# A fused gMLP / RWKV-7 layer on one core: the first superblock's modulation sums and the spatial weights change places with their neighbours

## The chip, the cores and the metric

The kernel runs on one core of one Trainium2 chip. The metric is device microseconds (us) of one execution. A core has TensorE (PE; its weight loads are shown as PEld), VectorE (DVE), ScalarE (ACT), GpSimd (POOL), and SyncE (SP), whose queue issues every DMA of this kernel.

## The reference, cut to what matters

x is 4096 x 1024. A conditioning vector c gives shift, scale and gate; h = x(1+scale)+shift is projected by one matrix w_in; columns 0 to 1535 feed head group A (u, v, gate), the rest head group B.

```python
shift, scale, gate = split(silu(c) @ w_ada + b_ada)
h = x * (1 + scale) + shift
p = h @ w_in
# group A: 8 groups of 64, chunks of 128
u = gelu(p[:, :512]);  v = layer_norm(gelu(p[:, 512:1024]));  g = silu(p[:, 1024:1536])
w_m = where(causal, w_spatial, 0)
v = einsum('gts,bcsgd->bctgd', w_m, v) + b_spatial
out_a = u * v * g
# group B: token shift, decay from tanh(wd) @ w_up, rate from ad @ a_up, RWKV-7 scan, group norm, silu gate
y = layer_norm(ALPHA * x + gate * (concat(out_a, out_b) @ w_out))
```

## The kernel before, in words

The sequence is cut into 16 superblocks of T = 256 tokens. Every float32 operand of a dense product is held as two rounded parts, hi and lo: `split` casts the source to hi on ACT and subtracts hi from the source on POOL or DVE. A dense block is 8 steps of k; one step is a matmul of 512 columns (L370, weight hi against x hi and lo) and one of 256 (L371, weight lo against x hi).

**Stage one** (0 to about 866 us, lines 456 to 664) runs head group A and the gate and decay columns of group B for all superblocks, with their weights resident. Superblock 0 also loads those weights. Its opening works on the input in halves of k: `first_half(a)` issues the loads of four 1 MB pieces of w_ada (`wa`), two x tiles and one 1 MB piece of w_in (`ust`); `second_half(a)` splits `ust` into the u weights, forms the sums silu(c) @ w_ada with `ada_sum` (16 small matmuls of L329 per 512 columns, a copy by DVE at L491, 8 matmuls of L493 that turn the row into columns of `pmod`), builds scale and shift in `mod`, and modulates and splits the x tiles. `group_a(0)` allocates one PSUM tile for each of the four u blocks, runs k = 0 to 3 of all four (`dense`), then calls `second_half(1)`, then runs k = 4 to 7.

The generator `weights` is advanced one step beside each step of `group_a(0)`: it loads the gate weights (`w_g`, four blocks), then the v weights (two 1 MB pieces `vst`, split into `wv`), then the `w_gb` blocks and `w_wd`, and last the spatial weights: a load of `wm` (512 KB), a mask on POOL (`affine_select`, L545), eight broadcast loads of b_spatial into `cb` (L549, called `bsp` in the rows) and 16 matmuls into `pR` (L553), which make the constant part of the spatial bias. After the u blocks, `group_a` runs the four gate blocks, two v products `psv` (L598 to L600), the `w_gb` blocks, `w_wd`, and the spatial product `pM` (L638).

In stage one the framework's scheduler chooses each engine's order from the order of the program and its own model of readiness; each engine then runs its queue strictly in order. All DMAs wait in SP's queue in order too.

**Stage two** (to about 2180 us) runs head group B twice over the 16 superblocks, two head pairs at a time (`ph` 0 and 1). The order of PE, DVE, ACT and POOL is written out at build time by a list planner, `Weave`: streams yield operations, each has a modelled cost, and the one that can start first is emitted next. A load's modelled due time is set by `W.load`. `dense` (line 861) calls `setup(ph)` at the first superblock of each `ph`: it loads w_up and a_up into two tiles taken from the two-buffer ring `pv` that the token shift also uses, casts them (`wua`) and subtracts. **The output projection** follows to the end.

Of the kernel before, what the change touches and what calls it, by code (L numbers as in the profile page):

```python
# [11 lines left out]
F32 = mybir.dt.float32  # L12
F32R = mybir.dt.float32r
AF = mybir.ActivationFunctionType
ALU = mybir.AluOpType
# [4 lines left out]
P = 128  # L20
# [189 lines left out]
def hybrid_layer(ctx: ExitStack, tc: tile.TileContext, x, xT, w_ada, b_gate, w_in, cols,  # L210
                 consts, wspT, b_sp, w_up, a_up, w_out, ln_g, ln_b, out):
    nc = tc.nc
    v, s, g, pe = nc.vector, nc.scalar, nc.gpsimd, nc.tensor
# [84 lines left out]
    def slices(hls):  # L298
        return [hl[:, :, k] for hl in hls for k in range(2)]
# [165 lines left out]
    with ExitStack() as actx:  # L465
# [20 lines left out]
        def ada_sum(q, parts):  # L486
            pq = ps_m.tile([P, 512], F32, tag="m", name="pq")
            for k in range(KD):
                group_row(pq, sg1, k, parts[k // 4][:, k % 4])
            rows = apool.tile([P, 512], F32, tag="wst", name="rows", bufs=3)  # L490
            v.tensor_copy(rows, pq)  # L491
            for mm in range(4):
                pe.matmul(pm[:, q * 4 + mm:q * 4 + mm + 1], rows[:, mm * P:(mm + 1) * P], row32,  # L493
                          start=True, stop=True)
# [8 lines left out]
            ld(st, w_in[a * 512:(a + 1) * 512, 0:512].rearrange("(k p) c -> p k c", p=P))  # L503
            half[a] = wa, xs, st

        def second_half(a):
            wa, xs, st = half[a]
            for b in range(4):
                split(wu[b][:, 0, 4 * a:4 * a + 4], wu[b][:, 1, 4 * a:4 * a + 4], st[:, :, b * P:(b + 1) * P], v)
            for n, q in enumerate((2 + a, a)):  # L510
                ada_sum(q, wa[n])
            sc, sh = slice(8 + 4 * a, 12 + 4 * a), slice(4 * a, 4 * a + 4)
            v.scalar_tensor_tensor(mod[:, sc], pm[:, sc], 1.0, V[:, V_BA + sc.start:V_BA + sc.stop], op0=ALU.add,
                                   op1=ALU.add)
            v.tensor_tensor(mod[:, sh], pm[:, sh], V[:, V_BA + sh.start:V_BA + sh.stop], op=ALU.add)
            return [modulate(2 * a + n, x_, (v, g)[n]) for n, x_ in enumerate(xs)]
# [7 lines left out]
        def weights():  # L524
            for b in range(4):
                wgt.append(load_w(2 * DA + b * P, f"w_g{b}", None if b < 3 else w2, (g, v)[b % 2], (None, apool)[b % 2]))
                yield
            vst = []
            for r in range(2):
                t_ = w2.tile([P, 4, DA], F32, tag="w", name=f"vst{r}")  # L530
                ld(t_, w_in[r * 512:(r + 1) * 512, DA:2 * DA].rearrange("(k p) c -> p k c", p=P))
                vst.append(t_)
            for k in range(KD):
                split(wv[:, 0, k], wv[:, 1, k], vst[k // 4][:, k % 4], (g, v)[k % 2])
            yield
            for b in range(4):
                wgb.append(load_w(NA + 1536 + b * P, f"w_gb{b}", w2, (g, v)[b % 2], (None, apool)[b % 2]))
                yield
            wwd.append(load_w(NA + 2048, "w_wd", w2))
            yield  # L540
            ones = apool.tile([P, 64], F32, name="ones", bufs=1)
            g.memset(ones, 1.0)
            ld(wm, wspT)

            g.affine_select(wm, wm, pattern=[[0, 8], [1, P]], compare_op=ALU.is_ge, fill=0.0, base=0,  # L545
                            channel_multiplier=-1)
            for b in range(4):
                for gi in range(2):
                    ld(cb[64 * gi:64 * gi + 64, b], b_sp[2 * b + gi:2 * b + gi + 1].partition_broadcast(64))  # L549
            pR = ps_m.tile([P, 4, P], F32, tag="m", name="pR")  # L550
            for b in range(4):
                for gi in range(2):
                    pe.matmul(pR[64 * gi:64 * gi + 64, b], ones, wm[:, 2 * b + gi], start=True, stop=True)  # L553
            for b in range(4):
                v.scalar_tensor_tensor(cb[:, b], pR[:, b], col(V_LB, b), cb[:, b], op0=ALU.mult, op1=ALU.add)
            yield

        def group_a(i):
# [7 lines left out]
            if i:  # L566
                h = load_all(i)
                yield
                for b in range(4):
                    gelu_u(gemm(h, wu[b]))  # L570
                    yield
            else:
                pus = [(ps_d if b < 2 else ps_s).tile([P, 2, T], F32, tag="ddss"[b], name="psd") for b in range(4)]
                for b in range(4):
                    dense(pus[b], slices(hl0), wu[b], 0, 4)
                hl0.extend(second_half(1))
                h = slices(hl0)
                yield
                for b in range(4):
                    dense(pus[b], h, wu[b], 4, KD)  # L580
                    gelu_u(pus[b])
                    yield
                keep_parts(0, hl0)
# [199 lines left out]
    with ExitStack() as bctx:  # L783
# [21 lines left out]
        def rsqrt_b(dst, src, bias_):  # L805
            yield ac.activation(dst, src, AF.Ln, bias=bias_)
            yield ac.activation(dst, dst, AF.Exp, scale=-0.5)

        def setup(ph):

            wua = W.tile(tp, [P, 4, 256], F32R, "wua", 1)
            yield gp.memset(wua[:, 2:4].bitcast(F32), 0.0)
            for q, src in enumerate((w_up, a_up)):
                r_ = slice(64 * q, 64 * q + 64)
                up = W.tile(tp, [P, 257], F32, "pv", 2, "up")[:, 0:256]
                for r in range(2):
                    W.load(up[64 * r:64 * r + 64], src[:, ph * 256:(ph + 1) * 256])
                yield ac.copy(wua[:, q], up)
                yield gp.tensor_tensor(wua[r_, 2 + q], up[r_], wua[r_, q].bitcast(F32), op=ALU.subtract)
            R[ph] = wua  # L820
# [40 lines left out]
        def dense(hs):  # L861
            u, p = divmod(hs, 2)
            ph, i = divmod(u, NSB)
            if p == 0:
                if ph not in R:
                    yield from setup(ph)
                units[u] = {}
                wd = W.tile(tp, [P, 2, T], F32R, "wd", 1)
                W.load(wd.bitcast(F32), wds[i])
                for _ in state["h"][1]:  # L870
                    pass
                state["cur"] = state["h"][0]
                state["side"] = iter(())
                if u == NSB - 1:
                    state["side"] = load_b1()
                elif u == NU - 1:
                    state["side"] = load_out()
            wua, h, n = R[ph], state["cur"], 2 * ph + p
            blocks = [("k", 4 + n), ("r", n), ("v", 8 + n)]

            for group in ([blocks[:1], blocks[1:]] if p else [[z_] for z_ in blocks]):
                pss = [W.tile(ps_d, [P, T], F32, "d", 3, "psd") for _ in group]
                fresh = len(group) > 1 and u + 1 < NU
                if fresh:
                    state["h"] = reload_parts((u + 1) % NSB)
                for k in range(KD):
                    hi, lo = h[k]
                    for (nm, blk), ps in zip(group, pss):
                        w = R[ph, nm, p]
                        yield [mm.matmul(ps, w[:, 0, k], hi, start=(k == 0), stop=False),  # L890
                               mm.matmul(ps, w[:, 0, k], lo, start=False, stop=False),
                               mm.matmul(ps, w[:, 1, k], hi, start=False, stop=(k == KD - 1))]
                    if k % 2 and fresh:
                        next(state["h"][1], None)
                for (nm, blk), ps in zip(group, pss):
                    t_ = W.tile(tp, [P, T], F32, nm, 2, nm + "t")
                    units[u][nm, p] = t_
                    W.spawn(shift_b(hs, nm, ps, blk, t_, n), 1.5)
                    next(state["side"], None)
                if nm == "k" and p == 0:  # L900
                    pw = []
                    for q in range(2):
                        pw.append(W.tile(ps_d, [P, 2, T], F32, "d", 3, "pw"))
                        yield [mm.matmul(pw[q][:, j], wua[:, q + 2 * z_, j * P:(j + 1) * P], wd[:, q],
                                         start=(z_ == 0), stop=(z_ == 1)) for j in range(2) for z_ in range(2)]
                    units[u]["sa"] = sas[u % 2]
                    W.spawn(rates(u, sas[u % 2], pw), 1.5)
                elif late and W.ready[late[0][1].tensor.name][0] <= W.clock["pe"]:
                    yield from put_late(ps_d, "d", 3)
            if p == 1:  # L910
                for _ in state["side"]:
                    pass
# [356 lines left out]
```

## Time and profile before

| | us |
|---|---|
| three runs | 2526.94, 2514.21, 2527.01; median 2526.94 |
| the profiled execution | 2518.34, span 2516.3 |
| busy: PE / DVE / ACT / POOL | 2382.3 / 1587.8 / 1266.3 / 761.0 |
| mean granted TensorE clock | 0.983 of full |

PE is busy for 95% of the span, so the time that can be won without removing matmuls is PE's idle time and the time that it runs at the lower of its two clocks. The timeline shows one instruction or a merged run of the same kind per line: start, duration, engine, line, operation, operands, count, and in brackets how long the engine was idle before it and what ended the wait.

### The profile page before, as it was taken

How to read it: one execution, taken by the hardware profiler on the slowest of the kernel's cores; microseconds unless marked ns; L12 is line 12 of the kernel's file. 1: busy time of each engine (PE TensorE's matmuls, PEld its weight loads, DVE VectorE, ACT ScalarE, POOL GpSimd, SP SyncE). 2: the span in 40 equal slices, each digit the busy share in tenths (PEclk: the TensorE clock that was granted, in tenths of full speed). 3: DMA queues.
4: the chain of work that ended last, by engine and by line, in shares of the span. 5: the costliest groups of instructions: out<-in, count | busy, mean ns of one | idle time of the engine just before them, and what ended most of it. 6: DMA issues, size and time to landing. Idle time of an engine off the chain costs nothing.

```text
span 2516.3 us, 57908 instructions
## 1 busy us (share of the span) xinstructions
PE 2382.3 (95%) x22676; PEld 2081.1 (83%) x22676; DVE 1587.8 (63%) x4205; ACT 1266.3 (50%) x2946; POOL 761.0 (30%) x1417
## 2 busy tenths in 40 slices
PE   7999999999999899999999989999999988899998
PEld 4778888888888798888888888888888887688887
DVE  4444545554344268778788777777877777555555
ACT  3444544454445565666666656566665555211111
POOL 2322433232222333332323333333333233222221
PEclk9999999999999999999999999999999899999999
DMA  8533455443223523222222342222212124344442
GB/s 299 172 122 122 149 178 180 159 147 113 72 72 105 168 77 90 75 71 85 60 86 71 123 137 64 86 69 77 90 56 85 56 77 161 110 147 143 150 148 95
DMA packets 182074, 286.14 MB, mean 114 GB/s; under 512 B 14500, under 2 KB 123172, under 8 KB 180008
## 3 DMA queue, kind: packets, MB, share of 16 engines
q1 hardware_dynamic: 181800, 282.44, 34.6%
q8 instruction: 178, 2.92, 0.5%
q14 instruction: 96, 0.79, 0.1%
HBM read 188.00 MB, written 94.38 MB: 112 GB/s over the span
## 4 chain that ended last, share of the span: by engine, by line
PE 60%; DVE 17%; ACT 7%; issue 4%; DMA 3%; POOL 2%; SPq 1%; DVEq 0%; POOLq 0%; ACTq 0%
PE pso L1221 13%; PE psd L166 12%; PE psd L370 9%; PE psd L371 5%; PE pU L166 3%; PE pC L166 3%; PE pA L166 2%; DVE big L166 2%; PE psv L598 2%; PE psv L600 2%; PE psv L599 2%; DVE X L166 2%; DVE tmp L166 2%; DVE S L166 1%; PE pY L166 1%
## 5 line engine op out<-in xcount | busy, mean ns | idle before, releaser
L1221 PE MATMUL pso<-wo,hx 128*128 128x512 f32 x1440 | 330.5, 391 | 1.8 <-POOL hx L1221 1.3
L1221 PEld LDWEIGHTS pso<-wo,hx 128*128 128x128 f32 x1440 | 270.3, 188 | 60.5 <-POOL hx L1221 1.7
L166 PE MATMUL psd<-hx,w_v 128*128 128x256 f32 x1512 | 251.0, 293 | 11.7 <-DVE kt L166 5.5
L166 PE MATMUL psd<-hx,w_r 128*128 128x256 f32 x1512 | 251.1, 292 | 2.7 <-issue 1.4
L166 PE MATMUL psd<-hx,w_k 128*128 128x256 f32 x1512 | 237.5, 298 | 4.9 <-DVE rt L166 4.9
L166 PEld LDWEIGHTS psd<-hx,w_v 128*128 128x128 f32 x1512 | 204.6, 192 | 17.7 <-DVE kt L166 7.1
L381 DVE TENSOR_TENSOR sum<-psd,sum 128x256 f32<-128x256 f32 x208 | 87.4, 421 | 195.1 <-ACT sum L380 195.0
L166 PEld LDWEIGHTS psd<-hx,w_r 128*128 128x128 f32 x1512 | 205.2, 191 | 6.2 <-DVE kt L166 2.1
L166 PEld LDWEIGHTS psd<-hx,w_k 128*128 128x128 f32 x1512 | 202.0, 197 | 7.3 <-DVE rt L166 6.0
L370 PE MATMUL psd<-hx,w_u 128*128 128x512 f32 x512 | 187.7, 409 | 6.2 <-ACT w_u L258 5.8
L370 PE MATMUL psd<-hx,w_gb 128*128 128x512 f32 x512 | 183.4, 400 | 0.5 <-DVE sum L381 0.5
L370 PE MATMUL psd<-hx,w_g 128*128 128x512 f32 x512 | 182.1, 399 | 0.5 <-DVE sum L381 0.5
L1221 POOL TENSOR_TENSOR hx<-hst,hx 128x512 fp32r<-128x512 f32 x58 | 81.8, 1412 | 221.5 <-ACT hx L1221 219.7
L371 PE MATMUL psd<-hx,w_u 128*128 128x256 f32 x512 | 145.8, 285 | 1.2 <-DVE w_u L259 1.2
L371 PE MATMUL psd<-hx,w_gb 128*128 128x256 f32 x512 | 144.9, 283 | 0.0
L371 PE MATMUL psd<-hx,w_g 128*128 128x256 f32 x512 | 143.8, 281 | 0.0
L166 ACT ACTIVATE pv<-psd,V 128x256 f32<-128x256 f32 x192 | 89.6, 474 | 98.1 <-PE psd L166 95.8
L166 POOL COPY halo<-pv 128x1 f32<-128x1 f32 x192 | 39.2, 205 | 315.0 <-ACT pv L166 308.0
L1221 DVE SCALAR_TENSOR_TENSOR z<-z,pso 128x512 f32<-128x512 f32 x60 | 41.2, 687 | 146.6 <-PE pso L1221 146.5
L380 ACT COPY sum<-psd 128x256 f32<-128x256 f32 x208 | 75.7, 365 | 107.4 <-PE psd L371 107.1
L370 PEld LDWEIGHTS psd<-hx,w_u 128*128 128x128 f32 x512 | 98.2, 192 | 34.0 <-ACT w_u L258 6.0
L259 POOL TENSOR_TENSOR hx<-hst,hx 128x512 fp32r<-128x512 f32 x62 | 79.7, 1294 | 128.9 <-ACT hx L258 128.9
(222 smaller groups left out, 5906.0 us busy)
## 6 DMA issues: line engine op xcount, KB each, us to landing
hx<-xhl SPq DMA_DIRECT2D x126, 512.0 KB, 4.1
xhl<-hx SPq DMA_DIRECT2D x64, 512.0 KB, 2.9
hst<-in_xT_dram SPq DMA_DIRECT2D x64, 256.0 KB, 3.5
hst<-oT SPq DMA_DIRECT2D x64, 256.0 KB, 2.9
z<-in_x_dram SPq DMA_DIRECT2D x32, 512.0 KB, 3.5
out_dram<-z SPq DMA_DIRECT2D x32, 512.0 KB, 2.6
wst<-in_w_in_dram SPq DMA_DIRECT2D x42, 256.0 KB, 3.6
wa<-in_w_ada_dram SPq DMA_DIRECT2D x8, 1024.0 KB, 12.0
```

The lines of the kernel that those rows point to most:

```text
L166: fn(*a, **k)
L259: eng.tensor_tensor(lo, src, hi.bitcast(F32), op=ALU.subtract)
L370: pe.matmul(ps, w[:, 0, k], both, start=(k == 0), stop=(k == KD - 1), skip_group_check=True)
L371: pe.matmul(ps[:, 0], w[:, 1, k], both[:, 0], start=False, stop=(k == KD - 1), skip_group_check=True)
L380: s.copy(t_, ps[:, 1])
L381: v.tensor_tensor(t_, ps[:, 0], t_, op=ALU.add)
L598: pe.matmul(ps, hi[:, js], wv[:, 0, k], start=(k == 0), stop=False)
L599: pe.matmul(ps, hi[:, js], wv[:, 1, k], start=False, stop=False)
L600: pe.matmul(ps, lo[:, js], wv[:, 0, k], start=False, stop=(k == KD - 1))
L1221: fn(*a, **k)
```

## The change

Three edits. (1) `second_half` takes a callable `beside` that it calls after the two `ada_sum`s and before `mod` is built; `group_a(0)` runs k = 0 to 3 of u blocks 0 and 1 before `second_half(1)` and hands it k = 0 to 3 of blocks 2 and 3. (2) In `weights`, the load of `wm`, its mask, and the eight loads of `cb` move from the last step to the step of the v weights, ahead of the two `vst` loads; the `pR` matmuls stay where they were. (3) `setup` no longer loads w_up and a_up: a new `fetch_low(ph)` loads them into one tile of their own, called at unit 0 for `ph` 0 and at unit 15, one unit before it is needed, for `ph` 1.

```diff
-        def second_half(a):
+        def second_half(a, beside=lambda: None):
...
             for n, q in enumerate((2 + a, a)):
                 ada_sum(q, wa[n])
+            beside()
             sc, sh = slice(8 + 4 * a, 12 + 4 * a), slice(4 * a, 4 * a + 4)
...
+            ones = apool.tile([P, 64], F32, name="ones", bufs=1)
+            g.memset(ones, 1.0)
+            ld(wm, wspT)
+
+            g.affine_select(wm, wm, pattern=[[0, 8], [1, P]], compare_op=ALU.is_ge, fill=0.0, base=0,
+                            channel_multiplier=-1)
+            for b in range(4):
+                for gi in range(2):
+                    ld(cb[64 * gi:64 * gi + 64, b], b_sp[2 * b + gi:2 * b + gi + 1].partition_broadcast(64))
             vst = []
...
             wwd.append(load_w(NA + 2048, "w_wd", w2))
             yield
-            ones = apool.tile([P, 64], F32, name="ones", bufs=1)
-            g.memset(ones, 1.0)
-            ld(wm, wspT)
...
             pR = ps_m.tile([P, 4, P], F32, tag="m", name="pR")
...
-                for b in range(4):
-                    dense(pus[b], slices(hl0), wu[b], 0, 4)
-                hl0.extend(second_half(1))
+
+                part = slices(hl0)
+                for b in range(2):
+                    dense(pus[b], part, wu[b], 0, 4)
+
+                def beside():
+                    for b in range(2, 4):
+                        dense(pus[b], part, wu[b], 0, 4)
+
+                hl0.extend(second_half(1, beside))
...
+        def fetch_low(ph):
+            up = W.tile(tp, [P, 2, 256], F32, "up", 1)
+            for q, src in enumerate((w_up, a_up)):
+                for r in range(2):
+                    W.load(up[64 * r:64 * r + 64, q], src[:, ph * 256:(ph + 1) * 256])
+            R["up", ph] = up
+
         def setup(ph):
...
-                up = W.tile(tp, [P, 257], F32, "pv", 2, "up")[:, 0:256]
-                for r in range(2):
-                    W.load(up[64 * r:64 * r + 64], src[:, ph * 256:(ph + 1) * 256])
+                up = R["up", ph][:, q]
...
             if p == 0:
+
+                if u in (0, NSB - 1):
+                    fetch_low((u + 1) // NSB)
                 if ph not in R:
```

## Rows read from the trace of the kernel before

**Rows 1.** Windows: length, busy us (instructions) by engine, clock, DMA share, GB/s.
```profile
100.00:200.00 100.00, 99.19 (x540) 77.93 (x539) 43.38 (x139) 39.87 (x77) 18.79 (x33) 1.00 0.36 119
...
1460.00:1475.00 15.00, 10.56 (x134) 9.18 (x132) 7.36 (x23) 8.05 (x24) 7.09 (x16) 0.77 0.63 198
...
1700.00:1800.00 100.00, 97.29 (x1427) 89.44 (x1414) 80.21 (x228) 68.61 (x174) 36.12 (x83) 1.00 0.25 76
1800.00:1900.00 100.00, 91.57 (x1284) 84.05 (x1282) 78.82 (x228) 60.29 (x154) 31.93 (x74) 0.97 0.26 79
```

**Rows 2.** Timeline of PE in the opening, 12 to 43 us.
```profile
29.99 0.46 PE L370 MATMUL psd<-hx,w_u 128*128 128x512 f32 x1
...
32.92 2.78 PE L329 MATMUL pq<-wa,sg 128*32 128x512 f32 x24
...
38.59 1.05 PE L493 MATMUL pmod<-K,rows 128*128 128x1 f32 x8 [0.88 <-DVE rows L491]
42.55 0.79 PE L370 MATMUL psd<-hx,w_u 128*128 128x512 f32 x1 [2.91 <-ACT w_u L258]
```

**Rows 3.** Timeline of ACT just before that.
```profile
41.88 2.18 ACT L258 CAST w_u<-ust 128x512 fp32r<-128x512 f32 x4
```

**Rows 4.** Timeline of SP, 0 to 130 us (time and total length of a run of issues).
```profile
46.25 2.62 SPq L269 DMA_DIRECT2D wst<-in_w_in_dram  x2
48.92 1.05 SPq L531 DMA_DIRECT2D vst<-in_w_in_dram  x2
...
71.16 0.50 SPq L543 DMA_DIRECT2D wm<-in_wspT_dram  x1
71.71 6.40 SPq L549 DMA_DIRECT2D bsp<-in_b_sp_dram  x8
```

**Rows 5.** DMA issues, 0 to 130 us: count, size of each, us from issue to landing.
```profile
vst<-in_w_in_dram SPq DMA_DIRECT2D x2, 1024.0 KB, 8.6
wm<-in_wspT_dram SPq DMA_DIRECT2D x1, 512.0 KB, 6.5
```

**Rows 6.** Timelines of POOL, ACT and DVE, 55 to 79 us, in order of time.
```profile
55.31 2.99 POOL L259 TENSOR_TENSOR wv<-vst,wv 128x512 fp32r<-128x512 f32 x2 [2.19 <-ACT wv L258]
...
58.43 2.17 ACT L258 CAST wv<-vst 128x512 fp32r<-128x512 f32 x4
...
59.58 3.38 DVE L259 TENSOR_TENSOR wv<-vst,wv 128x512 fp32r<-128x512 f32 x2 [0.73 <-ACT wv L258]
62.89 0.74 DVE L381 TENSOR_TENSOR sum<-psd,sum 128x256 f32<-128x256 f32 x2
...
78.08 1.09 POOL L545 TENSOR_SCALAR_AFFINE_SELECT wm<-wm 128x1024 f32<-128x1024 f32 x1
```

**Rows 7.** Timeline of PE, 63 to 99 us.
```profile
63.35 0.49 PE L598 MATMUL psv<-wv,hx 128*128 128x512 f32 x1 [0.99 <-DVE sum L381]
...
74.66 0.40 PE L370 MATMUL psd<-hx,w_gb 128*128 128x512 f32 x1
79.23 1.97 PE L553 MATMUL pR<-wm,ones 128*64 128x128 f32 x16 [4.18 <-POOL wm L545]
...
84.72 0.40 PE L370 MATMUL psd<-hx,w_gb 128*128 128x512 f32 x1
...
93.91 0.39 PE L370 MATMUL psd<-hx,w_wd 128*128 128x512 f32 x1
...
96.83 1.97 PE L638 MATMUL pM<-wm,vg 128*64 128x128 f32 x32
```

**Rows 8.** Timelines of ACT, SP and PE around the two calls of `setup`.
```profile
874.00 0.40 ACT L166 CAST wua<-up 128x256 fp32r<-128x256 f32 x1 [7.87 <-DMA up<-in_w_up_dram]
...
1464.38 1.11 SPq L84 DMA_DIRECT2D up<-in_w_up_dram  x2
...
1468.80 0.40 ACT L166 CAST wua<-up 128x256 fp32r<-128x256 f32 x1 [3.11 <-DMA up<-in_w_up_dram]
...
1471.06 1.22 PE L166 MATMUL pU<-rhs,yt 128*128 128x128 f32 x4 [3.07 <-ACT rhs L166]
```

More of the change, by code (lines that the diff above doesn't have):

```diff
@@ L540, in weights @@
             yield
-            ones = apool.tile([P, 64], F32, name="ones", bufs=1)
-            g.memset(ones, 1.0)
-            ld(wm, wspT)
-            g.affine_select(wm, wm, pattern=[[0, 8], [1, P]], compare_op=ALU.is_ge, fill=0.0, base=0,
-                            channel_multiplier=-1)
-            for b in range(4):
-                for gi in range(2):
-                    ld(cb[64 * gi:64 * gi + 64, b], b_sp[2 * b + gi:2 * b + gi + 1].partition_broadcast(64))
             pR = ps_m.tile([P, 4, P], F32, tag="m", name="pR")
@@ L573, in group_a @@
                 pus = [(ps_d if b < 2 else ps_s).tile([P, 2, T], F32, tag="ddss"[b], name="psd") for b in range(4)]
-                for b in range(4):
-                    dense(pus[b], slices(hl0), wu[b], 0, 4)
-                hl0.extend(second_half(1))
+                part = slices(hl0)
[5 more added lines that the diff above has]
+                hl0.extend(second_half(1, beside))
                 h = slices(hl0)
@@ L812, in setup @@
             yield gp.memset(wua[:, 2:4].bitcast(F32), 0.0)
-            for q, src in enumerate((w_up, a_up)):
+            for q in range(2):
                 r_ = slice(64 * q, 64 * q + 64)
-                up = W.tile(tp, [P, 257], F32, "pv", 2, "up")[:, 0:256]
-                for r in range(2):
-                    W.load(up[64 * r:64 * r + 64], src[:, ph * 256:(ph + 1) * 256])
+                up = R["up", ph][:, q]
                 yield ac.copy(wua[:, q], up)
```

## The prediction

> **What bounds the kernel now.** I read the windows first, to see where PE is not the limit, then PE's timeline for its idle brackets, then the queues that release those waits. From 100 to 200 us PE is busy 99.2 of 100 us [rows 1], and the later windows of stage one look the same, so stage one is bound by PE: a microsecond won in the first 100 us is not swallowed before stage two. The reader should look for three places where PE stands still. At 42.55 PE waits 2.91 us for the cast of the u weights, the end of the modulation chain [rows 2]. At 79.23 it waits 4.18 us for the mask of the spatial weights [rows 7]. At 1471.06, in the start of the second half of stage two, it waits 3.07 us behind ACT, which itself stood 3.11 us for the load of w_up [rows 8]. The change has one edit for each.
>
> **Edit 1, the modulation sums.** Blocks 2 and 3 of the first half-products run from 29.99 to 32.92, 2.93 us [rows 2]. The sums start at 32.92 and their last matmul ends at 38.59 + 1.05 = 39.64; the modulation, the casts (that of the u weights at 41.88 [rows 3]) and so the wait of 2.91 us follow. If PE does the sums right after block 1, the chain starts 2.93 us earlier and the two blocks fill its gaps; PE restarts at 42.55 - 2.93 = 39.62. The blocks then cover the idle time almost wholly (2.91 + 0.88 of idle against 2.93 of work), so PE should not fall to the lower clock either. What that clock costs I take from the other restart: after the 4.18 us of waiting, PE runs at half speed from the end of pR at 81.2 to 84.72 [rows 7], 3.5 us, which costs half of it, 1.75 us. Here part of it hides under the wait for the splits of the u weights, so I take 1.1 (bounds 0 and 1.75). Edit 1 brings 2.93 + 1.1 = 4.0 us at the end of the u blocks. No engine gets more work, and the transfers that the sums need were issued long before; that they have landed at 29.99 no row shows, only that they had by 32.92, where PE does not wait. If they had not, the gain is 0 (rival C).
>
> **Edit 2, the spatial weights.** What it removes: PE's wait of 4.18 us; pR at half speed (16 matmuls in 1.97 us, where pM does 32 of the same shape in 1.97 us [rows 7], so 0.98 too much); and the slow restart of 1.75. Together 6.9 us. The mask itself takes 1.09 us on POOL [rows 6]; in its new place it stands before the splits of the v weights, where POOL sat idle for 2.19 us, so it is free there, and uncovered it costs 1.09. The wm load takes 6.5 us to land [rows 5] and has some 20 us until pR. After it nothing on PE is late: the next block after psv has its weights split by then (L370 at 74.66 had begun before the wait [rows 7]).
>
> What it adds: nine issues on SP ahead of the two `vst` loads. One wm issue takes 0.50 us and the eight broadcasts 6.40 us [rows 4]; that last figure holds waits. The bounds are nine times 0.50 = 4.5, and 0.50 + 6.40 = 6.9. Behind them in SP's queue stand vst, the stores of the split x and all w_gb loads. The two `wst` loads before vst end at 48.87 [rows 4]; they wait for splits that move 2.93 us earlier with edit 1, so vst is issued between 46.0 + 4.5 = 50.5 and 52.9, against 48.92: 1.6 to 4.0 us later, although the rest of the stage is earlier. The second vst piece is cast at 58.43 and the last of its splits ends at 59.58 + 3.38 = 62.96 [rows 6]; this becomes 64.6 to 67.0. PE would be ready for psv at 63.35 - 0.99 - 4.0 = 58.4. So edit 2 takes back part of edit 1. The two psv products run from 63.35 to 74.66, 11.3 us for 48 matmuls, 0.236 each; psv 0 needs 5.65 and ends at 69.0 now. If it follows the splits as they come, only its last step of three matmuls, 0.7, is left after the last split: it ends at 65.3 to 67.7, a gain of 1.3 to 3.7. I take the middle, 2.5, for edit 1 and the late vst together.
>
> The Trainium skill (DMA: Bandwidth & Descriptors, section "Issuing engines are not separate DMA queues") says that the sequencer's time to start a DMA is usually small beside the DMA. By that rule the nine issues would cost little, edit 1's 4.0 us would survive whole, and the sum would be 1.5 higher. The rows do not agree for these eight: 6.40 us of issuing for 32 KB each.
>
> **Edit 3, w_up and a_up.** At the second `setup` the load is issued at 1464.38 and ACT waits until 1468.80; the cast stands ahead of the scan's copies on ACT, so PE waits 3.07 us [rows 8]. Loaded one unit earlier, this wait goes. The window 1460 to 1475 has a clock of 0.77 [rows 1]: 0.23 x 15 / 0.5 = 6.9 us at half speed, of which about 4.5 were idle, so at most 1.2 more comes back. I take 3.1, bounds 1.5 (half is lost to the next wait) and 4.3. The four loads are the same, only earlier. At the first `setup` ACT waits 7.87 us until 874.00 for the same loads [rows 8], but there nothing is issued earlier, since `fetch_low(0)` is called just ahead of `setup(0)`: I count 0. The `pv` ring is freed of two tiles. But the planner sees other due times from its first step on, so the order of all four engines in stage two can come out differently; no row prices that. The nearest are two neighbouring windows of the same work, in which PE is busy 97.3 and 91.6 us of 100 [rows 1]: 5.7 us between a good and a bad stretch of the same plan. I take 0, with 5 either way.
>
> **Sum.** 2.5 + 6.9 + 3.1 = 12.5 us. The profiled execution took 2518.34, so 2505.8 on that scale. It lies 8.6 below the median of the three runs and 4.1 above the lowest; the mean of all four executions is 2521.6, and 2521.6 - 12.5 = 2509. I predict 2510. A difference under 0.5%, 12.6 us, is about what a measurement of this kernel cannot tell from no change; the forecast sits right at that border.
>
> **Rivals.**
> A, the queue on DVE does not follow. Now the sums of gate blocks 1 and 2 (62.89) stand behind DVE's splits of the v weights, and psv 0 waits for the PSUM tile that they free [rows 6, 7]. If this order stays and vst comes 1.6 to 4.0 us later, psv 0 starts at 65.0 to 67.4 instead of 63.35, after some 7 us of idle, with a slow restart of 1.75: a loss of 3.4 to 5.8, middle 4.6. Total -4.6 + 6.9 + 3.1 = 5.4 gained: 2512.9 on the profile's scale. For it: it is the order of now. Against it: the framework chose that order with vst early, and chooses again. The same loss comes if the vst data queue behind wm's 512 KB on the DMA engines. The Trainium skill (DMA: Bandwidth & Descriptors, section "Queues, rings and completion order") says that descriptors on one engine are consumed in ring order, which would put them there; no row shows the two in flight together.
> B, everything is kept. wm and the broadcasts go out in a gap where SP waits anyway, vst is not late, and edit 1 keeps 4.0 and the 0.99 us at 63.35; edit 3 brings 4.3. 4.0 + 1.0 + 6.9 + 4.3 = 16.2: 2502.1. Against it: the framework would have had such gaps for wm before, and did not use them (wm at 71.16 [rows 4]).
> C, edit 1 does not do what it says: the framework's model finds the w_ada pieces not ready after block 1 and lets blocks 2 and 3 go first, as now. Then vst is 4.5 to 6.9 late, psv 0 ends at 68.2 to 70.6 against 69.0, a loss of 0.4 in the middle; -0.4 + 6.9 + 3.1 = 9.6: 2508.7.
> D, slower: the planner's new order is worse. It decides once it loses more than 12.5, a little over twice the 5.7 us between the two windows; three such stretches would cost 17 and end 4.6 above now: 2522.9. For it: the first due times change at the first unit, and 32 units follow. Against it: only two calls of `setup` are changed, and the streams and their costs stay.
>
> **How the numbers follow.** Forecast 0.48, A 0.20, B 0.12, C 0.10, D 0.10. The forecast's own range is 1.3 + 5.15 + 1.5 = 8.0 (edit 2 without the 1.75 of the clock) to 3.7 + 6.9 + 4.3 = 14.9 gained, so 2503.4 to 2510.4 on the profile's scale. The runs lie 4.1 below to 8.7 above that scale: 2499 to 2519; A ends at 2521.6 with the same 8.7 added, and a mild D a few above that: 2499 to 2525. Faster by over 0.5%: four tenths of the forecast (0.20), nearly all of B (0.11), and a lucky plan in the others (0.05): 0.36. Slower by over 0.5%: the far half of D, 0.05. Within: 0.59.
>
> **What would show it.** In the profile after: the L329 sums directly after eight L370/L371 pairs, and the second half's first L370 near 39.6, not 42.55; wm and bsp before vst on SP, and vst issued at 50.5 to 53; psv 0 starting before 63.35 in short pieces (forecast) or after 65 (A); pR without a wait and at about 1 us; the clock at full from 60 to 100; no ACT wait for `up` near 1460, and the start of stage two some 9 us earlier. The prediction is wrong if vst's delay reaches past 4 us, if another wait takes pR's place before pM, or if the stretch from 880 to 2180 changes its length by more than 5 us.

## The result and the profile after

The changed kernel takes 2502.97 us (median of six runs, 2499.14 to 2508.60) against 2522.74 (six runs, 2514.21 to 2527.01): ratio 0.9922, 95% interval 0.9905 to 0.9939, so 19.7 us or 0.78% shorter, where 12.5 were predicted. The time lies in the predicted range, but it is faster by more than half a per cent, to which the prediction gave a chance of 0.36; and most of the gain came from a place that the prediction had costed at 0. The profiled execution took 2503.15 (span 2501.4, clock 0.986), 15 us less than that of before.

**The opening did not do what edit 1 says.** Timeline of PE in the changed kernel; the rows of before are [rows 2]:

```profile
30.62 1.06 PE L329 MATMUL pq<-wa,sg 128*32 128x512 f32 x8
31.61 0.50 PE L370 MATMUL psd<-hx,w_u 128*128 128x512 f32 x1
...
32.39 1.06 PE L329 MATMUL pq<-wa,sg 128*32 128x512 f32 x8
33.39 0.39 PE L371 MATMUL psd<-hx,w_u 128*128 128x256 f32 x1
...
35.70 1.06 PE L329 MATMUL pq<-wa,sg 128*32 128x512 f32 x8
...
37.80 1.06 PE L329 MATMUL pq<-wa,sg 128*32 128x512 f32 x8
39.74 1.34 PE L493 MATMUL pmod<-K,rows 128*128 128x1 f32 x8 [0.88 <-DVE rows L491]
43.99 0.79 PE L370 MATMUL psd<-hx,w_u 128*128 128x512 f32 x1 [2.91 <-ACT w_u L258]
```

The first sum (the rows at 30.62 and 32.39) is ahead, but the matmuls of blocks 2 and 3 stand among the sums, nearly all of them ahead of the second one (35.70 and 37.80). The chain that ends the stall starts at the end of the last sum, and the wait of 2.91 us is there as before: PE restarts at 43.99, which is 19.4 us after its first u matmul, against 18.8.

**SP and PE around the spatial weights** (for [rows 4] and [rows 7]); the second fence is PE:

```profile
45.21 0.50 SPq L531 DMA_DIRECT2D wm<-in_wspT_dram  x1
47.69 2.61 SPq L269 DMA_DIRECT2D wst<-in_w_in_dram  x2
50.35 5.02 SPq L537 DMA_DIRECT2D bsp<-in_b_sp_dram  x8
55.42 1.14 SPq L541 DMA_DIRECT2D vst<-in_w_in_dram  x2
```

```profile
75.61 1.09 PE L554 MATMUL pR<-wm,ones 128*64 128x128 f32 x16
...
89.08 0.39 PE L370 MATMUL psd<-hx,w_wd 128*128 128x512 f32 x1
...
91.94 1.97 PE L646 MATMUL pM<-wm,vg 128*64 128x128 f32 x32
...
96.35 0.50 PE L370 MATMUL psd<-hx,w_u 128*128 128x512 f32 x1 [0.83 <-POOL hx L259]
```

pR now runs in 1.09 us without a wait. `vst` goes out 6.5 us later than before, more than the 4 that the prediction allowed, but psv starts 39.7 us after the first u matmul, as before (39.6): DVE now has gate sums ahead of and among its splits of the v weights (rows at 59.39 and 65.18 us). PE is 4.8 us earlier at w_wd. Some of that goes in superblock 1 (0.83 above, 0.28 once more for hx, 1.51 for gst where before had 0.72).

**Stage two.** Two tables from here on are worked out from rows. In this one a unit's marker is its first `pw` matmul, read from rows like this one of before (first and last start after the durations), unit 16:

```profile
L166 PE MATMUL pw<-wd,wua x8: 277/279/388, 1477.1 to 1479.7; 128*128 128x256 f32 x8
```

us from marker to marker; the last column is from unit 31 to the end of the span. "Order" is that of PE, DVE, ACT and POOL in stage two; "loads" are those of w_up and a_up for `ph` 1.

| kernel | order, loads | 0 to 4 | 4 to 15 | 15 to 16 | 16 to 24 | 24 to 31 | to the end |
|---|---|---|---|---|---|---|---|
| before | old, late | 128.8 | 427.9 | 44.6 | 311.0 | 290.6 | 437.6 |
| after | new, early | 132.1 | 427.7 | 40.7 | 311.5 | 276.3 | 440.5 |
| e3_prefetch | new, early | 128.8 | 429.0 | 39.2 | 311.5 | 275.9 | 440.9 |
| e4_same_plan | old, early | 129.1 | 429.0 | 40.4 | 310.6 | 286.6 | 438.1 |
| e7_late_loads | new, late | 129.4 | 427.9 | 44.7 | 314.3 | 277.4 | 440.6 |
| p64_half_piece | old, late | 127.1 | 433.4 | 47.0 | 314.6 | 265.3 | 439.5 |
| p128_whole_piece | old, late | 129.2 | 429.8 | 45.7 | 308.9 | 294.2 | 437.7 |
| a64_half_piece | new, early | 127.1 | 432.1 | 41.7 | 310.8 | 275.2 | 438.4 |

After against before, from the first marker: unit 0 starts 3.2 earlier; units 0 to 4 give 3.3 back; the second setup brings 3.9; units 24 to 31 bring 14.3; 2.9 are lost behind them. The setup is what edit 3 was for. Units 24 to 31 are the planner's new order, the term of 0.

### The profile page after: what moved, and what is told of

Read it like the earlier page. It is cut to its first block, busy times and chain, and to the rows that moved or that the text cites. A ratio compares the mean times of both kernels' runs of the same rounds, so it can differ in the third digit from the quotient of the medians.

```text
span 2501.4 us, 57879 instructions
## 1 busy us (share of the span) xinstructions
PE 2376.8 (95%) x22676; PEld 2072.6 (83%) x22676; DVE 1578.3 (63%) x4205; ACT 1269.0 (51%) x2946; POOL 757.0 (30%) x1417
## 4 chain that ended last, share of the span: by engine, by line
PE 53%; DVE 20%; ACT 8%; issue 5%; DMA 3%; POOL 2%; SPq 1%; DVEq 0%; ACTq 0%; POOLq 0%
PE pso L1237 13%; PE psd L166 10%; PE psd L370 9%; PE psd L371 5%; PE pU L166 3%; PE pC L166 2%; DVE big L166 2%; PE pA L166 2%; DVE X L166 2%; PE psv L606 2%; PE psv L608 2%; PE psv L607 2%; DVE tmp L166 2%; DVE S L166 2%; ACT sa L166 1%
## 5 line engine op out<-in xcount | busy, mean ns | idle before, releaser
L166 PE MATMUL psd<-hx,w_k 128*128 128x256 f32 x1512 | 231.2, 293 | 9.2 <-DVE rt L166 7.8
L166 PEld LDWEIGHTS psd<-hx,w_k 128*128 128x128 f32 x1512 | 196.0, 192 | 13.6 <-DVE rt L166 9.7
L1237 POOL TENSOR_TENSOR hx<-hst,hx 128x512 fp32r<-128x512 f32 x59 | 84.4, 1432 | 222.9 <-ACT hx L1237 221.0
L370 PEld LDWEIGHTS psd<-hx,w_gb 128*128 128x128 f32 x512 | 96.2, 188 | 26.4 <-DVE sum L381 1.1
```

What stands on the lines that cost most here:

```text
L166: fn(*a, **k)
L370: pe.matmul(ps, w[:, 0, k], both, start=(k == 0), stop=(k == KD - 1), skip_group_check=True)
L1237: fn(*a, **k)
```

## The experiments

### Each edit alone

e1_sums, e2_spatial and e3_prefetch are the kernel before with edit 1, 2 or 3, as in the diff; e9_both has edits 1 and 2.

> Edit 1 alone (blocks 2 and 3 of the half products handed to `second_half` as `beside`), nothing else changed. Theory I (read from the two traces): the framework puts half of blocks 2 and 3 ahead of the second sum on PE, so the restart of the u blocks comes some 1.4 us later than before instead of 2.9 earlier; stage one ends 0 to 2 us later and the total is 0 to 2 us longer than the kernel before. Rival (the prediction's own sum): the edit brings up to 4 us where vst is not late, so the total is 2.5 to 4 us shorter.

Measured: 1.0018 of the kernel before (1.0000 to 1.0036), 4.5 us longer by the middle of the interval. No gain; the prediction's 2.5 to 4 us are excluded.

> Edit 2 alone (wm, mask and the eight broadcast loads ahead of the two vst loads). Theory: pR loses its wait of 4.18 us and its half speed, worth 6.9 in the prediction; vst goes out some 5 us later than before, so that psv starts up to 2 us later, and part of what is left is given back in superblock 1, where PE then waits for hx and for gst; 2 to 5 us shorter than the kernel before. Rival: the whole 6.9 stays. Rival on the other side: the late vst takes all of it, within 1 us of before.

Measured: 0.9987 (0.9967 to 1.0007), 3.3 us shorter by the middle of the interval. pR has no wait, and PE reaches w_wd 5.5 us earlier.

> Edit 3 alone (`fetch_low`). Theory II: the edit does two things, it takes the wait of 3 to 5 us out of the second setup, and it lets the planner choose another order of stage two, worth another 8 to 9 us after 1500 us; the total is 11 to 14 us shorter than the kernel before, 85% or more of what the whole change brings. Rival (the prediction's term): only the wait goes, 3.1 us (1.5 to 4.3); then edits 1 and 2 must bring some 16.

Measured: 0.9948 (0.9927 to 0.9968), 13 us (8 to 18). This one edit carries two thirds of the change.

> Edits 1 and 2 without edit 3, with the old order of stage two. From the traces: the two bring 3 to 4.5 us by the start of stage two, 3 of which are lost again in its fourth unit (an "issue" wait of 1.8 instead of 1.3 us at about 990, and PE at the lower clock behind it), so 0 to 3 us shorter than the kernel before. If they bring 5 or more here, the difference between the whole change (0.9922) and edit 3 alone (0.9948) is theirs; if not, that difference is within what the two intervals leave open.

Measured: 0.9985 (0.9961 to 1.0010), 3.8 us, from 9.8 shorter to 2.5 longer. Edit 3's 13 and these 3.8 make 17, and the whole change's interval is 15 to 24: the parts add up within what the runs can tell.

### Edit 3 taken apart: the early loads or the new order

The planner works from names and due times that it is told, so either half of edit 3 can be had without the other. e4_same_plan loads early and tells the planner the old ring and due time; e7_late_loads loads in `setup` and tells it the new due time. In both, the order of PE, DVE, ACT and POOL is row for row that of the kernel before or of edit 3 alone; only SP's differs.

```diff
 # e4_same_plan: fetch_low loads into tiles of its own, unseen by the planner; in setup
+                up = R["up", ph][q]
+                ring = W.rings.setdefault((id(tp), "pv"), [])
+                ring.append(up.tensor.name)
+                if len(ring) > 2:
+                    W.after[up.tensor.name] = ring[-3]
+                W.ready[up.tensor.name] = W.now + 2000.0 + 64 * 256 * 0.02, None
...
 # e7_late_loads: fetch_low only notes the due time; in setup
+            R["due", ph] = W.now + 2000.0 + 64 * 256 * 0.02
...
+                up = tp.tile([P, 257], F32, tag="pv", name="up", bufs=2)[:, 0:256]
+                for r in range(2):
+                    nc.sync.dma_start(up[64 * r:64 * r + 64], src[:, ph * 256:(ph + 1) * 256])
+                W.ready[up.tensor.name] = R["due", ph], None
```

> Edit 3's loads (issued early, into tiles of their own) with the planner told the due times and the ring of the kernel before, so that PE, DVE, ACT and POOL keep their old order in every row and only SP's differs. Theory II: the wait at 1468 goes, and no more: 3 to 5.5 us shorter than the kernel before. If the early loads alone give 10 or more, the order has no part in it; if they give under 1, the wait was hidden after all and the order is everything.

> The reverse of the one before: the planner is told edit 3's due times, so that PE, DVE, ACT and POOL stand in the order that edit 3 gives them, while the loads are issued in `setup` into `pv` tiles, as before the change. Theory II: the order is worth 8 to 9 us by itself, the wait at the second setup stays (3 us or more): 6 to 9 us shorter than the kernel before. If the order is worth nothing by itself, this runs within 2 us of the kernel before.

Measured: the early loads alone 0.9997 (0.9978 to 1.0017); the order alone 0.9951 (0.9936 to 0.9966), 12 us, all of edit 3. The cast of `wua` on ACT, in e4_same_plan and then in e7_late_loads, which answers to the row at 1468.80 in [rows 8]:

```profile
1469.49 0.41 ACT L166 CAST wua<-up 128x256 fp32r<-128x256 f32 x1
```

```profile
1471.88 0.40 ACT L166 CAST wua<-up 128x256 fp32r<-128x256 f32 x1 [3.15 <-DMA up<-in_w_up_dram]
```

So the wait goes exactly where the loads are early, and in the traces that shortens the stretch from unit 15 to 16 by 5.4 us whatever the order (five traces with early loads have 39.2 to 41.7, mean 40.5; nine with late loads 44.4 to 47.2, mean 45.9). In the time of e4_same_plan's twelve runs these microseconds do not show: 0.8 of gain, from 5.5 shorter to 4.3 longer. What takes them back, if anything does, one trace of that kernel does not tell; it stays open.

### Why the new order is faster

Units 24 to 31 hold it. PE's waits there in the kernel before, from its timeline, all with the mark "issue", for which the profile knows no releaser:

```profile
1819.59 0.62 PE L166 MATMUL psd<-hx,w_v 128*128 128x256 f32 x3 [1.81 <-issue]
1858.46 0.61 PE L166 MATMUL psd<-hx,w_r 128*128 128x256 f32 x3 [1.38 <-issue]
1900.54 0.96 PE L166 MATMUL psd<-hx,w_v 128*128 128x256 f32 x3 [1.91 <-issue]
1942.48 0.49 PE L166 MATMUL pA<-AR,BK 64*128 64x128 f32 x3 [1.61 <-issue]
1982.67 1.22 PE L166 MATMUL pA<-AR,BK 64*128 64x128 f32 x6 [1.47 <-issue]
2027.42 0.82 PE L166 MATMUL pA<-AR,BK 64*128 64x128 f32 x9 [1.15 <-issue]
2067.99 1.65 PE L166 MATMUL pA<-AR,BK 64*128 64x128 f32 x12 [2.78 <-issue]
```

One in each unit, 12.1 us together. All six traces with the old order taken up to here have these seven, 10.7 to 13.9 us; the four with the new order have 0.2 to 0.7. SP shows what each follows: a burst of three or four hx loads of 512 KB, issued from 1811 us on in every unit. The last burst before a wait, and what the DMA queues carried from 2060 to 2068:

```profile
2058.43 0.33 SPq L316 DMA_DIRECT2D hx<-xhl  x1
...
2060.49 1.77 SPq L316 DMA_DIRECT2D hx<-xhl  x2
```

```profile
q1 hardware_dynamic: 930, 1.71, 66.7%
q8 instruction: 1, 0.02, 0.7%
```

A packet of the queue "instruction" lies inside the burst. Over the whole span that queue moved this (both kernels; the page's section on DMA queues):

```profile
q8 instruction: 178, 2.92, 0.5%
```

PE's instructions in the trace of before are 22676 matmuls, 22676 weight loads and 239 of its sequencer: 45591, or 256 for each of the 178 packets, which makes 64 bytes each. So this queue brings PE its program, in blocks of 256 instructions. The Trainium skill (Runtime: NRT & Kernel Launch, section "Instruction fetch mechanics") says the same of the size, and that the cost of crossing from one block to the next is mostly hidden; the rows above are where it is not.

The traces' records, which have the start and end of each instruction and each packet, settle that PE waits for these packets. Counted in PE's instructions (a matmul with its weight load is two), the seven waits stand exactly 1024 apart, four blocks. All 120 "issue" waits that PE has after 870 us in the fourteen traces stand at one place of a block: the instructions ahead of them, divided by 256, leave 192 or 193. And each of the 120 ends 1.19 to 1.62 us after a packet of this queue has landed. With 512 matmuls and as many weight loads a unit is close to four blocks, so a fetch that meets the hx burst in one unit meets it in the next.

What the bursts have to do with it is tested by moving the fetch. Spare matmuls at the end of stage one do only that (64 of them here, 128 in p128_whole_piece):

```diff
         s.copy(onesr, ones_blk)
+        spare = ps_m.tile([P, 512], F32, tag="m", name="spare")
+        for _ in range(64):
+            pe.matmul(spare[:, 0:128], onesr, onesr, start=True, stop=True)
```

With their weight loads 64 of them are 128 instructions more, half a packet, and 128 are 256, a whole one: the trace of p128_whole_piece has 179 packets. No engine's order changes otherwise.

> The kernel before with 64 spare matmuls (128x128, into a PSUM tile that nothing reads) on PE at the end of stage one: PE's program grows by 128 instructions, 8 KB, and nothing else changes in the order of any engine. In all six traces with the old order PE stands for 10.7 to 13.9 us, 7 times, on "issue" in the last seven units of stage two, each time behind a burst of hx loads, with two pieces of 16 KB on the instruction queue beside them; in the three new-order traces with early loads it stands 0.2 to 0.7 us. Theory III: PE waits there for the next piece of its own program, which is fetched by DMA behind the hx bursts, and the changed order helps because it moves the fetch against the bursts. Shifted by half a piece, the seven waits fall under 4 us in sum, the last seven units take 275 to 281 us instead of 283 to 292, and the total is 4 to 10 us shorter than the kernel before, if the shift makes no such meeting elsewhere. Rival: the waits belong to the old order itself; they stay at 10 us or more, and the total is that of before.

> The same with 128 spare matmuls: 256 instructions, 16 KB, one whole piece. Theory III: the fetches come at the same places of each unit as in the kernel before, so the seven waits stay (10 to 14 us in sum, 283 us or more for the last seven units) and the total is within 3 us of the kernel before. If the waits go here as with 64, it is not the phase of the fetch but the spare matmuls themselves (their effect on the start of stage two).

> The changed kernel with the same 64 spare matmuls. Theory III: the gain of the new order is one of phase; moved by half a piece, PE's fetches meet hx bursts again in some units, "issue" waits of more than 5 us come up in stage two and 4 us or more of the gain is lost against the changed kernel (0.994 to 0.998 of the kernel before instead of 0.992). Rival: the new order has spread its hx loads so that no phase of the fetch meets a burst; the time is that of the changed kernel within 2 us.

Measured: 64 spare matmuls make the kernel before **faster**, 0.9928 (0.9902 to 0.9954), 18 us; 128 leave it where it was, 1.0016 (0.9994 to 1.0038). Units 24 to 31 of before, p64_half_piece, p128_whole_piece and after in the windows view (length, then busy us of PE, PEld, DVE, ACT, POOL, then granted clock, DMA share, GB/s):

```profile
1788.10:2078.70 290.60, 268.54 (x3588) 247.04 (x3586) 214.81 (x609) 175.16 (x441) 90.30 (x210) 0.95 0.23 70
```

```profile
1800.70:2066.00 265.30, 254.53 (x3588) 234.92 (x3586) 213.99 (x609) 174.60 (x441) 91.08 (x210) 1.00 0.25 76
```

```profile
1795.60:2089.80 294.20, 269.91 (x3586) 248.17 (x3585) 214.71 (x609) 175.34 (x441) 91.04 (x210) 0.94 0.22 69
```

```profile
1784.60:2060.90 276.30, 262.30 (x3680) 240.50 (x3679) 217.38 (x624) 180.74 (x455) 88.52 (x215) 0.99 0.25 74
```

The waits of PE in the same stretch of p64_half_piece, the longest groups, and then of p128_whole_piece (total, times, longest):

```profile
PE psd L166 <- DVE kt L166: 4.2, 6, 0.7
PE pU L166 <- DVE UV L166: 2.2, 7, 0.3
...
PE pY L166 <- issue: 0.7, 2, 0.4
```

```profile
PE pA L166 <- issue: 7.7, 4, 2.0
PE psd L166 <- issue: 6.5, 3, 2.4
PE psd L166 <- DVE kt L166: 4.2, 6, 0.7
```

The reader should see three things. The half packet removes the waits (0.7 us for 12.1) and the whole packet leaves them, 14.2 us. (The half packet makes a few such meetings elsewhere, 4.3 us of "issue" up to the second setup and 5.4 in units 16 to 24, as the table's columns show; the total gains all the same, by more than was expected.) The hx bursts are still there in p64_half_piece; the DMA view of one, 2050 to 2058:

```profile
q1 hardware_dynamic: 866, 1.76, 70.8%
...
hx<-xhl SPq DMA_DIRECT2D x3, 512.0 KB, 4.5
```

A packet of instructions comes right behind this window, at 2058.30. So the half packet did not take the fetches out of the bursts; it changed how long PE's code in hand lasts while one is late. By the records, the DMA engines had been 75 to 98% busy for 4 us when the packets of the seven waits of before started. These landed 2.6 to 4.7 us after PE had started the block before the missing one, and that block, of short matmuls, lasted PE 2.7 to 4.1 us. In p64_half_piece, too, seven packets start behind engines 64 to 95% busy and land 3.2 to 4.2 us after that start, but there the block in hand lasts 5.0 to 5.6 us. In p128_whole_piece it lasts 2.7 to 4.1 again.

And the waits cost about twice their length. The same 3588 matmuls take 254.53 us of PE time where the clock is 1.00 and 268.54 where it is 0.95, so the 25.3 us between the two stretches are 14.0 of slower matmuls and 11.4 of waiting on "issue". The clock's records of before have four stretches at the lower level (1.2 GHz) there, from 1859.7, 1900.6, 1982.5 and 2067.9 us on, 30.7 us in all, each beginning between 0.2 us before and 1.3 us after the end of one of these waits; p64_half_piece has none.

a64_half_piece ran at 0.9934 (0.9910 to 0.9958), 3 us above the changed kernel by the ratios and within both intervals, with no "issue" wait in its units 24 to 31. There theory III was too strong and the rival nearer: the new order isn't only in a lucky phase. Its SP rows in the changed kernel have the hx loads of the last unit spread over 6 us, with other transfers between, instead of two in 1.8 us behind a third:

```profile
2044.44 0.33 SPq L316 DMA_DIRECT2D hx<-xhl  x1
...
2047.32 0.46 SPq L316 DMA_DIRECT2D hx<-xhl  x1
...
2050.08 0.42 SPq L316 DMA_DIRECT2D hx<-xhl  x1
```

By the count above, the changed kernel has three blocks in units 24 to 31 that last 2.9 to 4.3 us, as short as those of before; the packet due next, behind engines 47 to 65% busy, lands 1.4 to 2.9 us after their start, and PE waits 0.7 us in all. So in the changed kernel the spread fits. In a64_half_piece two packets come behind engines 80% busy again, landing 3.2 and 4.4 us after that start, and PE does not run out: the blocks there last 5.1 and 5.9 us. Two phases were tried, not all.

### Stage one: what the first two edits could bring

e5_forced is edit 1 with an ordering edge that holds blocks 2 and 3 behind the last sum; e6_wm_only is edit 2 with only `ones`, the `wm` load and the mask moved, the eight broadcasts left in place; e8_best has both of these and edit 3.

```diff
 # e5_forced, on top of edit 1: group_row and ada_sum return their last matmul
-            beside()
+            beside(last)
...
+                def beside(last):
+                    with tc.issue_after(last.ins):
+                        for b in range(2, 4):
+                            dense(pus[b], part, wu[b], 0, 4)
```

> Edit 1 alone, with an ordering edge that puts blocks 2 and 3 behind the last matmul of the second sum on PE, as the prediction had it. Theory: the pieces of w_ada have landed in time, the framework's model only believes they have not; the sums then run from about 29.7 to 34, the restart comes at 39.6 to 40.2 (before 42.55, edit 1 as compiled about 43.1 on the same scale), and PE is 2.4 to 4 us earlier at the end of the u blocks. Rival C in its hard form: the last piece of w_ada really lands after 34, PE waits for it in front of the two blocks, and the restart is no earlier than 42. On the total 0 to 4 us shorter than the kernel before, depending on how much the v weights let through.

> Half of edit 2: ones, the wm load and the mask go ahead of vst, the eight broadcast loads stay where the kernel before has them, behind w_wd. Theory: the 5.0 us that the broadcasts take on SP are what makes vst late; without them vst is issued within 1.5 us of 48.92, psv starts within 0.5 us of 63.35, pR still has no wait, and PE reaches w_wd 6 to 7 us earlier than 93.91 instead of 5. The total is 1 to 2 us shorter than that of edit 2 alone if superblock 1 lets it through, and the same as edit 2 alone if superblock 1 gives it back (its loads of hst and gst are then the limit).

> All that should help put together: edit 1 with its order forced, the mask early with the broadcasts left late, and edit 3. If the gains add, 2 to 6 us shorter than the changed kernel; if superblock 1 gives the first 100 us back, within 1.5 us of it.

PE's first u matmul comes between 23.0 and 26.4 us in the traces, with the opening loads, so the milestones are counted from it:

| us after the first u matmul | second half restarts | psv | wait before pR | w_wd | unit 0 of stage two |
|---|---|---|---|---|---|
| before | 18.8 | 39.6 | 4.18 | 70.2 | 852.1 |
| e1_sums | 19.5 | 41.1 | 3.56 | 70.1 | 851.9 |
| e5_forced | 15.2 | 32.9 | 6.09 | 65.1 | 848.5 |
| e2_spatial | 19.3 | 39.2 | 0 | 64.7 | 850.0 |
| e6_wm_only | 18.5 | 39.3 | 0 | 63.1 | 847.1 |
| after | 19.4 | 39.7 | 0 | 64.5 | 848.0 |
| e8_best | 15.8 | 33.5 | 0 | 58.2 | 845.0 |

In the last column e3_prefetch, e4_same_plan, e7_late_loads and p64_half_piece, whose stage one is that of before, have 852.0 to 853.2 (p128_whole_piece, with twice the spare matmuls, 856.8); a64_half_piece and e9_both, whose stage one is that of after, have 850.4 and 851.1 against its 848.0. So a single entry there is uncertain by some 3 us. The opening of e5_forced on PE:

```profile
31.97 2.78 PE L329 MATMUL pq<-wa,sg 128*32 128x512 f32 x24
...
35.69 1.06 PE L329 MATMUL pq<-wa,sg 128*32 128x512 f32 x8
...
41.60 1.03 PE L370 MATMUL psd<-hx,w_u 128*128 128x512 f32 x2 [0.92 <-ACT w_u L258]
```

Held in that order, the sums run straight through, so the w_ada pieces had landed by then; that the framework's model had put them later is argued, as no run shows that model's times. PE restarts 3.6 us earlier and comes to psv 6.7 earlier. By the clock of the device: e5_forced 0.9993 (0.9975 to 1.0011), e6_wm_only 0.9992 (0.9975 to 1.0010), e8_best 0.9917 (0.9890 to 0.9943; median 2500.72 of five). The 12.0 us that e8_best gains by w_wd are 7.1 at stage two, and its time cannot be told from the changed kernel's 0.9922. e6_wm_only issues vst at 47.88 and gains 1.5 more than e2_spatial at w_wd, as expected of it; in the runs the two cannot be told apart.

Where do such gains go? Part goes in superblock 1, which takes 59.0 us from w_wd to w_wd before, 61.3 in the changed kernel and 64.0 in e8_best; from there to the w_wd of superblock 15 all fourteen traces take 704.4 to 705.7. Another part shows in units 0 to 4, where the changed kernel gives back 3.3 us in one unit. PE's timeline there, before and then after:

```profile
993.85 0.29 PE L166 MATMUL pY<-yl,G 32*32 32x16 f32 x10 [1.30 <-issue]
```

```profile
990.97 0.30 PE L166 MATMUL pY<-yl,G 32*32 32x16 f32 x11 [1.79 <-issue]
```

Again an "issue" wait. From this unit's marker to the next PE is busy for 35.90 us of 38.9 at clock 1.00 before, and 38.90 of 42.4 at 0.92 after, for the same 512 and 513 matmuls.

## Why the prediction was right in the sum and wrong in its terms

**Edit 1** (4.0, with the late vst 2.5): it brought nothing, 1.0018 alone. The step "if PE does the sums right after block 1" failed: the order in which the program states them is not the order that the framework emits. That was rival C's mechanism, at a chance of 0.10. The working behind it was sound as far as PE's opening goes: under the forced order the restart moved by 3.6 (predicted 2.93), and psv by more than the 4.0 predicted for the end of the u blocks. The wait before pR then grew from 4.18 to 6.09, and e5_forced's time cannot be told from that of before.

**Edit 2** (6.9): right in mechanism and size, where it is clean. The mask alone brings 7.0 at w_wd, and the wait, pR's half speed and the slow restart all went. With the broadcasts 5.5 to 5.7: they do delay vst, by more than the bound of 4 us, but rival A's loss did not come, because DVE's order followed. What the sum lacked is the way from w_wd to the end: by the runs edit 2 alone is worth 3.3 us, with an interval that includes 0. That "a microsecond won in the first 100 us is not swallowed before stage two" held for superblocks 2 to 15, not for superblock 1 with its waits of 1.51 for gst and 1.11 for hx, nor for stage two's first units.

**Edit 3's wait** (3.1): 5.4 in the traces, above its upper bound of 4.3; in the runs of e4_same_plan not to be seen.

**Edit 3's new order** (0, with 5 either way): the step that failed. It measured 12 us (8.6 to 16) in e7_late_loads. The prediction had priced it by two neighbouring windows, 97.3 and 91.6 us busy of 100 [rows 1], and read their difference as good and bad stretches of one plan. The worse window holds two of the seven "issue" waits (1819.59 and 1858.46), most of a third (the 1.91 us up to 1900.54) and a clock of 0.97. Those waits, 12.1 us in seven, were in the trace of before to be read, each with a burst of loads beside it; the prediction did not ask what PE waited for where no releaser is named. The prediction named a change of more than 5 us between 880 and 2180 as what would prove it wrong: from unit 0 to unit 31 it is 14.6. Its bound of 4 us on the delay of vst was such a sign too, and it was passed by 2.5.

So the sum came out 7 us short of the runs and inside the range because terms erred both ways: the sums' 2.5 and part of the 6.9 did not come, and 12 came that were not counted. That the time lies in the range is in good part luck. Rival D had the right place, the planner's order, and the wrong sign. The prediction also took half a per cent for what a measurement of this kernel cannot tell from no change; the interval of this one is 0.17% either way.

## What to carry to other kernels

In a long unrolled program, read PE's "issue" waits beside SP's loads: if they recur at one point of every unit with a burst of transfers in front, PE may be waiting for its own code. The trace tells: such waits stand whole packets of instructions apart, and each ends just after a packet of the queue "instruction" has landed. Half a packet of spare instructions, with a whole packet as the control, then shows what it costs. When an edit also changes what an order-making planner is told, run the new order with the old loads and the old order with the new loads before crediting the loads. And an edit that only restates program order has to be read in the emitted order; here one ordering edge made the difference between nothing and 3.6 us at the restart.

## What the runs showed of the hardware that was not expected

Sixty-four matmuls that nobody reads made a kernel of 2522 us 18 us faster, and 128 did not. PE's code, 178 packets of 16 KB at 0.5% of the DMA engines' time, cost the kernel before 12.1 us of waiting in seven units, and the lower clock after these waits another 14 us of PE time. A packet that was late behind a burst cost a wait where the 256 instructions in hand lasted PE 2.7 to 4.1 us, and next to none where they lasted 5.0 to 5.6. One unit ran at clock 1.00 with an "issue" wait of 1.30 us and at 0.92 with one of 1.79.
